# Block 1's attention products as float32r parts: scores and P V on the whole array, with half-height heads stacked as [hi;lo]

## The chip, the cores and the metric

The kernel runs on one core of one Trainium2 chip. The metric is device time in microseconds. The core's engines are TensorE (PE; its loads of stationary tiles are listed as PEld), VectorE (DVE), ScalarE (ACT), GpSimd (POOL) and SyncE (SP), which here only issues DMAs.

## The reference

Two transformer blocks are applied to 256 tokens of 1024 features, in float32. The first block has two layers on 272 positions (16 meta tokens and the 256 tokens). Each layer normalizes, projects once (`u @ w_in`), runs four branches and merges them behind sigmoid gates, then a gated convolutional feed-forward net. The branches that matter here, with T = 272:

```
A: 4 heads, 2 maps each:  s[m] = q[m] k[m]^T / 8 + bias      (64 features a map)
   a = softmax(s[0]) - lambda * softmax(s[1]);   o = a v       (v has 128 columns)
B: gated linear attention in chunks of 64
C: 4 heads:  s = (q_nope k_nope^T + q_pe k_pe^T) / sqrt(192)  (128 and 64 features)
   o = softmax(s) v                                            (128 columns)
D: 8 query heads on 2 key heads, window 128, meta tokens always seen, a sink
   s = q k^T / 8 + bias (64 features);   o = softmax(s) v      (64 columns)
```

The second block (two SwiGLU nets a layer, retention and dilated attention, stick-breaking attention) is not touched in its arithmetic.

## The kernel before

Features lie on partitions, tokens in the free dimension. A weight matrix comes from DRAM in pieces of 1 MB (`load`, three buffers `raw`). Each 128 columns of it are split into a pair: `hi` is an ACT copy to float32r, `lo` is a DVE subtraction of `hi` from the raw value (`split`, L209). A dense product is then three float32r products, hi x hi, hi x lo and lo x hi (`mm3`, L183), accumulated in a PSUM bank; a chunk of 128 columns over 1024 features is 24 of them. The pairs rotate through a ring of four buffers for hi and four for lo (pool `hip`, L1622), for the whole kernel.

In the first block the attention products are not split. Their operands are plain float32, and TensorE runs such a product as two instructions with the same tiles:

- scores of A (L675) and D (L774): a stationary tile of 64 rows by 128 queries, 272 keys; the two maps of a head (A), or the two heads of a chunk (D), lie in rows 0 to 63 and 64 to 127;
- scores of C (L888, L889): one product with 128 rows and one with 64;
- P V (`weighted`, L600): three products with 16, 128 and 128 keys; 128 output rows for A and C, 64 for D.

The weights P are normalized in SBUF (tile `E`), transposed on TensorE against an identity (L191), and copied by DVE into the tile `PT` (`transposed`, L574: a 128 x 512 copy, a 16 x 256 one, and two small ones for the 16 meta queries). The meta tokens' queries of all heads are packed in one tile and done once a branch (`meta_weights`, L588). Their biases `bmA` and `bmD` are loaded once, from POOL's queue (L424 to L426). The other biases come per head or chunk on SP's queue into a ring of three buffers, `B` (L668, L762). `PT` has two buffers (pool `ptp`, L1133). The values are transposed to tokens (`values`, L562): a 16 x 128 and a 128 x 256 DVE copy for each 128 columns; branch B uses the same function.

The order of the work is written in `layer1` (L1120): branch B, the projections of A and of C's latents, A's attention, the merge of B, the projections of D, C's up-projections and attention, the merge of A, D's attention, the merges of C and D. A planner then orders each engine's instructions by when they can start and when they are needed, so that dense products of one branch stand between the attention steps of another. Each engine, and each DMA queue, carries out its own list in order; waits are on semaphores.

Of the kernel before, what the change touches and what calls it, by code (L numbers as in the profile page):

```python
# [12 lines left out]
F32 = mybir.dt.float32  # L13
# [20 lines left out]
# column offsets in w_in  # L34
# [8 lines left out]
# token tiles of the first block: the meta tokens, then two tiles of 128  # L43
# [3 lines left out]
# constants that depend on shapes alone, one tensor; name -> (first column, columns)  # L47
# [25 lines left out]
def _constants():  # L73
# [63 lines left out]
    put(c2, "strictadd", np.where(t_ < s_, 0.0, NEG).astype(f))  # queries on partitions  # L137
# [18 lines left out]
    # relative positions: bucket table as one-hot columns for rel = 272 - i  # L156
# [10 lines left out]
class _Kernel:  # L167
# [69 lines left out]
    def newton(self, y, h, u, x, scale, eps):  # L237
        """y = (scale * x + eps) ** -0.5"""
# [3 lines left out]
        # a step of third order, without its factor of 1.5, then one of second order  # L242
# [8 lines left out]
    def after(self, last):  # L251
        """What this traces on the engines of the instructions `last` is issued after them."""
# [21 lines left out]
    def pairs(self, raw, kc, cw, slots=(), eng=None):  # L274
        """Stationary tiles of 128 columns, split: [(hi, lo)], each [128, kc, 128]."""
# [8 lines left out]
    def weights(self, w, c0, cw, kc=NK, slots=(), eng=None):  # L284
        """Columns c0..c0+cw of w [kc*128, n], split, by 128 columns."""
# [3 lines left out]
    def chunk(self, w, x, n, ps=None):  # L289
        """PSUM [128, n] = w^T x"""  # L290
# [6 lines left out]
    def chunks(self, ws, x, n):  # L297
        """PSUM [128, n] = w^T x for each w, all of them as x comes."""
# [7 lines left out]
    def stream(self, ws, x, n, first=3, more=0, total=None, rs=None):  # L306
        """PSUM tiles of w^T x in turn; the first ones follow x as it comes, some more use the scores' banks."""
# [11 lines left out]
    def setup(self):  # L319
# [15 lines left out]
        # gains and other vectors, as columns of 128  # L335
# [19 lines left out]
    def setup_vectors(self):  # L355
        """Gains, biases and convolutions' weights, as columns; the second call transposes most of them."""
# [58 lines left out]
    def setup_tables(self):  # L415
# [3 lines left out]
        # biases of the meta tokens' queries, packed: rows 32 * group + 16 * member + query  # L419
        self.bmA = cp.tile([P, T], F32, tag="bmA", name="bmA")  # L420
        self.bmD = cp.tile([P, T], F32, tag="bmD", name="bmD")
        for g in range(4):
            r = slice(32 * g, 32 * g + 32)
            nc.gpsimd.dma_start(self.bmA[r, :], self.toeplitz(g, 0, 16, 0, T, [4 * 544, 2]))  # L424
            nc.gpsimd.dma_start(self.bmD[r, T - 16 :], self.toeplitz(8 + g, 0, 16, 0, 16, [4 * 544, 2]))
            nc.gpsimd.dma_start(self.bmD[r, : T - 16], self.toeplitz(24 + g, 0, 16, 16, T - 16, [4 * 544, 2]))  # L426

        # lambda of the differential attention, sinks
# [23 lines left out]
        for l in range(2):  # L452
            # 1 for the first map's rows, -lambda for the second's
# [5 lines left out]
            self.sinkcol.append(lam[:, 2 + l : 3 + l])  # L459

# [20 lines left out]
    def add_square(self, total, a, first, eng):  # L481
        """total (+)= a * a"""
# [7 lines left out]
    def mean_rsqrt(self, total, n, width):  # L490
        """[128, n]: (mean over the features + eps) ** -0.5 in each row, from the sums by partition."""
# [38 lines left out]
    def postnorm(self, chunks, gain, l, h):  # L530
        """What does h[m] += rms_norm(f) * gain; chunks yields (m, PSUM of f's 128 features)."""
# [26 lines left out]
    # slots of [128, 4, T]; a tag's tiles are placed in the order of the program, so what may run ahead  # L558
    # has its own
# [40 lines left out]
    def weighted(self, out, V, c, w, PT):  # L600
# [1077 lines left out]
```

## Time and profile before

| | |
|---|---|
| time, median of 3 runs | 2298.96 us (2297.48 to 2299.21) |
| span of the profiled execution | 2293.8 us |
| profiled execution's own time | not listed beside its span |
| PE busy | 2220.7 us, 97%, 16925 instructions |
| PEld busy | 2081.1 us, 91% |
| DVE busy | 1672.1 us, 73% |
| ACT busy | 1069.5 us, 47% |
| POOL busy | 264.5 us, 12% |
| mean granted TensorE clock | 0.989 of full speed |

Busy time is the union of an engine's instructions. Matmuls are pipelined, so one starts before the one before it has ended; the distance from start to start is then what an instruction costs. The times of stretches are microseconds from the start of the span. The first layer's attentions lie between 140 and 420, its feed-forward net between about 430 and 640; the second layer's between 760 and 1040 and between about 1050 and 1250.

### The profile page before, as it was taken

How to read it: one execution, taken by the hardware profiler on the slowest of the kernel's cores; microseconds unless marked ns; L12 is line 12 of the kernel's file. 1: busy time of each engine (PE TensorE's matmuls, PEld its weight loads, DVE VectorE, ACT ScalarE, POOL GpSimd, SP SyncE). 2: the span in 40 equal slices, each digit the busy share in tenths (PEclk: the TensorE clock that was granted, in tenths of full speed). 3: DMA queues.
4: the chain of work that ended last, by engine and by line, in shares of the span. 5: the costliest groups of instructions: out<-in, count | busy, mean ns of one | idle time of the engine just before them, and what ended most of it. 6: DMA issues, size and time to landing. Idle time of an engine off the chain costs nothing.

```text
span 2293.8 us, 41993 instructions
## 1 busy us (share of the span) xinstructions
PE 2220.7 (97%) x16925; PEld 2081.1 (91%) x16925; DVE 1672.1 (73%) x3263; ACT 1069.5 (47%) x1678; POOL 264.5 (12%) x329
## 2 busy tenths in 40 slices
PE   8999999899979999998999999999999999999998
PEld 6989779899979898798999999988999999979997
DVE  7867676799488776768985774787774775687764
ACT  5243334566443433346664553444543554445543
POOL 5100112133031001121320000101000100101000
PEclk9999999999989999999999999999999999999999
DMA  7255336355533543464555555544555555524553
GB/s 211 93 137 164 96 106 176 129 184 179 176 115 92 150 148 111 106 205 158 187 175 175 166 185 184 176 139 132 186 187 183 179 185 184 183 99 151 187 190 119
DMA packets 300741, 360.61 MB, mean 157 GB/s; under 512 B 17382, under 2 KB 265444, under 8 KB 300420
## 3 DMA queue, kind: packets, MB, share of 16 engines
q1 hardware_dynamic: 298652, 354.38, 48.7%
q0 software_dynamic: 1664, 3.48, 0.5%
q8 instruction: 133, 2.18, 0.4%
q14 instruction: 60, 0.49, 0.1%
q10 hardware_dynamic: 232, 0.08, 0.0%
HBM read 354.63 MB, written 1.12 MB: 155 GB/s over the span
## 4 chain that ended last, share of the span: by engine, by line
PE 82%; DVE 10%; ACT 3%; issue 2%; DMA 2%; POOL 1%; SPq 0%; ACTq 0%; DVEq 0%; POOLq 0%
PE acc L181 57%; PE att L181 23%; PE att L191 2%; DVE lo L212 2%; ACT hi L207 1%; POOL total L488 1%; DVE xl L204 1%; DVE c L204 1%; DVE f L201 1%; DVE h L201 1%; ACT xh L207 1%; DVE b L201 1%; DMA raw<-in_w_in_dram 0%; DVE b L204 0%; DVE total L488 0%
## 5 line engine op out<-in xcount | busy, mean ns | idle before, releaser
L207 ACT ACTIVATE hi<-raw 128x1024 fp32r<-128x1024 f32 (+1 forms) x651 | 677.4, 1045 | 840.2 <-PE acc L181 632.1
L212 DVE TENSOR_TENSOR lo<-raw,hi 128x1024 fp32r<-128x1024 f32 (+1 forms) x649 | 803.0, 1241 | 286.8 <-ACT hi L207 280.1
L181 PE MATMUL acc<-xh,lo 128*128 128x256 f32 (+2 forms) x3312 | 951.9, 288 | 2.1 <-DVE lo L212 2.1
L181 PE MATMUL acc<-xh,hi 128*128 128x256 f32 (+2 forms) x3312 | 952.7, 288 | 0.6 <-ACT hi L207 0.5
L181 PE MATMUL acc<-xl,hi 128*128 128x256 f32 (+2 forms) x3312 | 947.1, 286 | 0.1
L181 PEld LDWEIGHTS acc<-xh,hi 128*128 128x128 f32 x3312 | 629.4, 190 | 10.9 <-issue 7.5
L181 PEld LDWEIGHTS acc<-xh,lo 128*128 128x128 f32 x3312 | 628.4, 190 | 11.6 <-issue 7.7
L181 PEld LDWEIGHTS acc<-xl,hi 128*128 128x128 f32 x3312 | 631.0, 191 | 6.7 <-issue 5.3
L181 PE MATMUL att<-ah,hi 128*128 128x256 f32 (+1 forms) x704 | 199.6, 283 | 0.0
L181 PE MATMUL att<-al,hi 128*128 128x256 f32 (+1 forms) x704 | 199.5, 283 | 0.0
L181 PE MATMUL att<-ah,lo 128*128 128x256 f32 (+1 forms) x704 | 199.5, 283 | 0.0
L488 POOL TENSOR_TENSOR total<-total,sq 128x256 f32<-128x256 f32 (+2 forms) x60 | 58.4, 973 | 815.1 <-ACT sq L207 812.4
L181 PEld LDWEIGHTS att<-ah,lo 128*128 128x128 f32 x704 | 134.5, 191 | 0.0
L181 PEld LDWEIGHTS att<-al,hi 128*128 128x128 f32 x704 | 134.5, 191 | 0.0
L181 PEld LDWEIGHTS att<-ah,hi 128*128 128x128 f32 x704 | 134.5, 191 | 0.0
L1118 POOL TENSOR_TENSOR merged<-merged,gate 128x272 f32<-128x272 f32 (+1 forms) x48 | 56.6, 1180 | 525.7 <-DVE small L904 275.4
L181 PE MATMUL acc<-ol,hi 128*128 128x272 f32 (+2 forms) x384 | 112.4, 293 | 1.1 <-DVE ol L212 1.1
L181 PE MATMUL acc<-oh,hi 128*128 128x272 f32 (+2 forms) x384 | 111.7, 291 | 0.0
L181 PE MATMUL acc<-oh,lo 128*128 128x272 f32 (+2 forms) x384 | 111.0, 289 | 0.0
L204 DVE SCALAR_TENSOR_TENSOR c<-u,vec,c 128x272 f32<-128x272 f32 (+1 forms) x176 | 105.5, 607 | 2.5
L201 DVE TENSOR_TENSOR u<-acc,rs 128x256 f32<-128x256 f32 (+2 forms) x171 | 72.4, 426 | 46.7 <-PE acc L181 46.4
L181 PEld LDWEIGHTS acc<-ol,hi 128*128 128x128 f32 x384 | 72.5, 189 | 8.1 <-issue 6.3
(370 smaller groups left out, 3104.3 us busy)
## 6 DMA issues: line engine op xcount, KB each, us to landing
raw<-in_ffn_w_in_dram SPq DMA_DIRECT2D x88, 1024.0 KB
raw<-in_w_in_dram SPq DMA_DIRECT2D x64, 1024.0 KB
raw<-in_ffn_w_up_dram SPq DMA_DIRECT2D x44, 1024.0 KB
raw<-in_ffn_w_out_dram SPq DMA_DIRECT2D x44, 1024.0 KB
raw<-in_ffn_w_down_dram SPq DMA_DIRECT2D x20, 1024.0 KB
raw<-in_hyb_w_in_dram SPq DMA_DIRECT2D x14, 1024.0 KB
raw<-in_w_branch_dram SPq DMA_DIRECT2D x12, 1024.0 KB
raw<-in_sb_w_in_dram SPq DMA_DIRECT2D x12, 1024.0 KB
```

Source lines behind the costliest of these rows:

```text
L181: self.last_mm = self.nc.tensor.matmul(ps, lhsT=lhsT, rhs=rhs, start=start, stop=stop, skip_group_check=True)
L191: return self.nc.tensor.transpose(ps, a, self.ident[:n, :n])
L201: self.nc.vector.tensor_tensor(out, a, b, op)
L204: return self.nc.vector.scalar_tensor_tensor(out, a, s, b, op0, op1)
L207: return self.nc.scalar.activation(out, a, f, **kw)
L212: (eng or self.nc.vector).tensor_tensor(lo, a, hi.bitcast(F32), ALU.subtract)
L488: self.last_add = eng.tensor_tensor(total, total, sq, ALU.add)
L1118: self.nc.gpsimd.tensor_tensor(merged[m], merged[m], x, ALU.add)
```

## The change

Scores and P V of A, C and D become products of float32r parts.

- A and D: a half-height operand of the queries is stored as a full-height tile [hi; lo] (`halves`), each head's or map's own rows holding hi and the other 64 rows lo. The keys are stored twice, as [hi; hi] and [lo; lo] (`doubled`). Two full-height products give all four parts of the score.
- C: `mm3` for the 128-row part, and two products for the rotary part, with [hi; lo] queries against the two tiles of the rotary key, which holds equal rows in both halves.
- P V: `transposed` now makes `ph` by an ACT copy and `pl` by a DVE subtraction; the 16 meta keys of P are stacked in an 80-row tile (hi in rows 0 to 15, and hi and lo in rows 32 to 47 and 64 to 79), whose other rows are zero. `weighted` is one product for the meta keys and `mm3` for each of two key tiles, seven in all. For D the values are put in tiles 128 columns wide whose other 64 columns are zero, and both heads of a chunk accumulate in one bank.
- `values` splits likewise; branch B keeps the old function under the name `plain_values`. `meta_weights` returns split weights.
- The meta queries' biases are no longer kept: `meta_bias` loads them in each layer, on SP's queue, into the ring `B`.
- Buffers: `hip` has three buffers in the first block and is opened again with four for the second. `P^T` (now `PH`, `PL`) has one buffer each, and so have the operand halves (`half_tile`). C's packed meta scores issue their four 128-row products first, then the 64-row ones.

Comments are dropped throughout. The core of the diff:

```diff
@@ transposed, weighted
+        ph, pl = (self.ptp.tile([P, 2, T], F32R, tag=f"P{t}", name=self.name("P" + t)) for t in "HL")
+        self.pm = self.pm[::-1]
+        pm = self.pm[0]
...
-        cp(PT[:, 1:3, 16:T], tp.rearrange("p (k q) -> p k q", k=2))
-        cp(PT[:16, 0, 16:T], t0[:16, 0:256])
-        cp(PT[:, 1:3, 0:16], meta[:, 64:192].rearrange("p (k g q) -> p k g q", k=2, g=4)[:, :, h])
-        cp(PT[:16, 0, 0:16], meta[:16, 16 * h : 16 * h + 16])
+        main = tp.rearrange("p (k q) -> p k q", k=2)
+        self.act(ph[:, :, 16:T], main, AF.Copy)
+        self.tt(pl[:, :, 16:T], main, ph[:, :, 16:T].bitcast(F32), ALU.subtract)
+        self.meta_rows(pm[:, 16:T], t0[:16, 0:256], "hi")
+        mh, ml = meta
+        cp(ph[:, :, 0:16], mh[:, 64:192].rearrange("p (k g q) -> p k g q", k=2, g=4)[:, :, h])
+        cp(pl[:, :, 0:16], ml.rearrange("p (k g q) -> p k g q", k=2, g=4)[:, :, h])
+        cp(pm[:, 0:16], mh[:80, 16 * h : 16 * h + 16])
...
-        for kt, (a, n) in enumerate(TILES):
-            self.mm(out, V[:n, kt, c : c + w], PT[:n, kt, :], kt == 0, kt == 2)
+        vh, vl, vm = V
+        ph, pl, pm = PT
+        self.mm(out, vm[:, cs], pm, start, False)
+        for kt in range(2):
+            self.mm3(out, (vh[:, kt, cs], vl[:, kt, cs]), (ph[:, kt], pl[:, kt]), False, stop and kt == 1)
@@ new helpers
+    def meta_rows(self, out, a, second):
+        self.act(out[0:16], a, AF.Copy)
+        hi, lo = (slice(32, 48), slice(64, 80))[:: 1 if second == "hi" else -1]
+        self.tt(out[lo], a, out[0:16].bitcast(F32), ALU.subtract)
+        self.act(out[hi], a, AF.Copy)
+    def half_tile(self, tag):
+        return self.mw.tile([P, T], F32R, tag=tag, name=self.name(tag), bufs=1)
+    def halves(self, a, tag):
+        out = []
+        for m in range(2):
+            r, o = slice(64 * m, 64 * m + 64), slice(64 - 64 * m, 128 - 64 * m)
+            t = self.half_tile(f"{tag}{m}")
+            self.act(t[r], a[r], AF.Copy)
+            self.tt(t[o], a[r], t[r].bitcast(F32), ALU.subtract)
+            out.append(t)
+        return out
+    def doubled(self, a):
+        out = []
+        for m in range(2):
+            r, o = slice(64 * m, 64 * m + 64), slice(64 - 64 * m, 128 - 64 * m)
+            hi, lo = self.half_tile(f"kd{m}"), self.half_tile(f"kl{m}")
+            self.act(hi[r], a[r], AF.Copy)
+            self.tt(lo[r], a[r], hi[r].bitcast(F32), ALU.subtract)
+            self.act(hi[o], a[r], AF.Copy)
+            self.act(lo[o], lo[r].bitcast(F32), AF.Copy)
+            out.append((hi, lo))
+        return out
@@ branch_a (branch_d likewise, with ks = self.doubled(K) once)
+            qs, ks = self.halves(Q[:, h], "qs"), self.doubled(K[:, h])
...
-                    self.mm(ps[:, :T], Q[64 * m : 64 * m + 64, h, a : a + P], K[64 * m : 64 * m + 64, h, :])
+                    for t in range(2):
+                        self.mm(ps[:, :T], qs[m][:, a : a + P], ks[m][t], t == 0, t == 1)
@@ branch_c
+        kr = self.half_tile("kl0"), self.half_tile("kl1")
+        self.split(*kr, KR)
...
+            if h % 2 == 0:
+                qr = self.halves(QR[:, h // 2], "qr")
+            qn, kn = (tuple(self.half_tile(f"{tag}{n}") for n in range(2)) for tag in ("qs", "kd"))
+            self.split(*qn, QN[:, h])
+            self.split(*kn, KN[:, h])
...
-                self.mm(ps[:, :T], QN[:, h, a : a + P], KN[:, h], True, False)
-                self.mm(ps[:, :T], QR[r0 : r0 + 64, h // 2, a : a + P], KR[r0 : r0 + 64, :], False, True)
+                self.mm3(ps[:, :T], [q[:, a : a + P] for q in qn], kn, True, False)
+                for t in range(2):
+                    self.mm(ps[:, :T], qr[h % 2][:, a : a + P], kr[t], False, t == 1)
@@ branch_a, branch_d
-        self.neg_scores(em, ps[:, :T], self.bmA[:, ::-1], sm[:, 0:1])
+        self.neg_scores(em, ps[:, :T], self.meta_bias(0, False), sm[:, 0:1])
@@ layer1, run
-            self.ptp = self.pool(st, f"ptp{l}", 2, reuse_waits="tile")
+            self.ptp = self.pool(st, f"ptp{l}", 1, reuse_waits="tile")
-        self.hip = self.pool(ctx, "hip", 4)
+            self.hip = self.pool(block, "hip", 3, reuse_waits="tile")
+        self.hip = self.pool(ctx, "hip2", 4, reuse_waits="tile")
```

## Rows read from the trace of the kernel before

**Rows 1.** The page: span, and busy us (share of the span) xinstructions.

```profile
span 2293.8 us, 41993 instructions
...
PE 2220.7 (97%) x16925; PEld 2081.1 (91%) x16925; DVE 1672.1 (73%) x3263; ACT 1069.5 (47%) x1678; POOL 264.5 (12%) x329
```

**Rows 2.** Stretches: start:end length, busy PE, PEld, DVE, ACT, POOL, clock, DMA, GB/s.

```profile
140.00:187.00 47.00, 46.53 (x276) 34.80 (x276) 37.61 (x137) 22.24 (x53) 0.00 (x0) 1.00 0.49 121
760.00:805.00 45.00, 45.00 (x291) 34.88 (x290) 35.20 (x126) 21.77 (x51) 0.00 (x0) 1.00 0.52 137
...
140.00:420.00 280.00, 278.69 (x1905) 236.90 (x1905) 196.81 (x523) 118.07 (x224) 29.38 (x26) 1.00 0.47 136
760.00:1040.00 280.00, 277.22 (x1952) 235.93 (x1951) 198.51 (x529) 116.99 (x224) 28.17 (x25) 1.00 0.50 145
420.00:640.00 220.00, 207.62 (x1623) 205.67 (x1622) 177.32 (x270) 123.58 (x193) 54.17 (x59) 0.99 0.52 170
```

**Rows 3.** PE's old products: groups (busy us, mean ns), then P V's ns min/median/max.

```profile
L181 PE MATMUL att<-dk,b 64*128 64x272 f32 x64 | 17.6, 441 | 0.0
L181 PE MATMUL att<-b,b 64*128 64x272 f32 x64 | 16.7, 441 | 0.5 <-DVE small L613 0.5
L181 PE MATMUL att<-kr,b 64*128 64x272 f32 x32 | 11.6, 441 | 0.0
L181 PE MATMUL att<-b,b 128*128 128x272 f32 x32 | 10.7, 415 | 0.0
...
L181 PE MATMUL att<-PT,V x192: 387/393/497, 162.1 to 971.3; 128*128 128x272 f32 x64, 128*64 128x272 f32 x64, 16*128 16x272 f32 x32, 16*64 16x272 f32 x32
```

**Rows 4.** Timeline of PE in A's attention: start us, length us, instruction, count.

```profile
163.86 0.72 PE L181 MATMUL att<-b,b 64*128 64x272 f32 x2
...
167.49 1.84 PE L181 MATMUL att<-PT,V 16*128 16x272 f32 x6
169.25 0.73 PE L181 MATMUL att<-b,b 64*128 64x272 f32 x4
169.91 0.39 PE L181 MATMUL acc<-xh,lo 128*128 128x272 f32 x1
170.14 0.29 PE L181 MATMUL acc<-xh,hi 128*128 128x272 f32 x1
...
171.15 0.29 PE L181 MATMUL acc<-xh,lo 128*128 128x272 f32 x1
```

**Rows 5.** Timeline of PE in D's attention, one block of P V.

```profile
318.50 1.73 PE L181 MATMUL att<-PT,V 16*64 16x272 f32 x6
```

**Rows 6.** Groups of ACT and DVE: count, then busy us, mean ns, idle before.

```profile
L207 ACT ACTIVATE b<-merged 128x272 fp32r<-128x272 f32 x8 | 3.5, 432 | 16.8 <-POOL merged L1118 16.8
L1038 ACT COPY b<-att 128x512 f32<-128x512 f32 x8 | 4.7, 585 | 18.3 <-PE att L181 18.3
...
L201 DVE TENSOR_TENSOR gate<-acc,rs 128x272 f32<-128x272 f32 x32 | 13.9, 434 | 16.7 <-PE acc L181 16.7
L212 DVE TENSOR_TENSOR lo<-raw,hi 128x512 fp32r<-128x512 f32 x20 | 13.1, 688 | 0.8 <-ACT hi L207 0.6
L583 DVE COPY PT<-att 128x512 f32<-128x512 f32 x32 | 22.1, 690 | 12.6 <-PE att L191 12.4
L585 DVE COPY PT<-metaw 128x32 f32<-128x32 f32 x32 | 5.2, 162 | 0.0
```

**Rows 7.** Timelines of PE, ACT and DVE in the conv stage, about one pair.

```profile
504.01 0.29 PE L181 MATMUL acc<-xh,hi 128*128 128x272 f32 x1
...
504.64 1.04 ACT L207 ACTIVATE hi<-raw 128x1024 fp32r<-128x1024 f32 x1
...
506.11 1.73 DVE L212 TENSOR_TENSOR lo<-raw,hi 128x1024 fp32r<-128x1024 f32 x1
```

**Rows 8.** SP's waits (us, times, longest); the chain's longest bias landing in A's stage.

```profile
SPq L668 <- DVE small L613: 29.1, 5, 9.9
...
153.56 4.40 DMA B<-rel
```

More of the change, by code (lines that the diff above doesn't have):

```diff
@@ L459, in setup_tables, with meta_bias @@
             self.sinkcol.append(lam[:, 2 + l : 3 + l])
+    def meta_bias(self, row, masked):
+        b = self.bp.tile([P, 2, T], F32, tag="B", name=self.name("B"))[:, 0]
+        for g in range(4):
+            r = slice(32 * g, 32 * g + 32)
+            if masked:
+                self.nc.sync.dma_start(b[r, T - 16 :], self.toeplitz(row + g, 0, 16, 0, 16, [4 * 544, 2]))
+                self.nc.sync.dma_start(b[r, : T - 16], self.toeplitz(row + 16 + g, 0, 16, 16, T - 16, [4 * 544, 2]))
+            else:
+                self.nc.sync.dma_start(b[r, :], self.toeplitz(row + g, 0, 16, 0, T, [4 * 544, 2]))
+        return b[:, ::-1]
     def k(self, name):
@@ L560, with token_values, zeros, values @@
     SLOTS = {"b4": 8, "E": 2, "ms": 1, "oh": 1, "ol": 1}
-    def values(self, V, c, ps, rs, n):
+    def token_values(self, ps, rs):
+        vt = self.mw.tile([P, T], F32, tag="vt", name=self.name("vt"))
+        self.tt(vt, ps, rs, ALU.mult)
+        tp = self.att()
+        for j in (1, 2, 0):
+            a, w = TILES[j]
+            self.transpose(tp[:w, (j + 2) % 3 * P : ((j + 2) % 3 + 1) * P], vt[:, a : a + w])
+        return tp
+    def meta_rows(self, out, a, second):
[3 more added lines that the diff above has]
+        self.act(out[hi], a, AF.Copy)
+    def zeros(self, pool, shape, tag, **kw):
+        t = pool.tile(shape, F32R, tag=tag, name=self.name(tag), **kw)
+        self.nc.gpsimd.memset(t.bitcast(F32), 0.0)
+        return t
+    def values(self, V, c, ps, rs):
+        tp = self.token_values(ps, rs)
+        cs = slice(c * P, (c + 1) * P)
+        main = tp[:, : 2 * P].rearrange("p (j v) -> p j v", j=2)
+        self.act(V[0][:, :, cs], main, AF.Copy)
+        self.tt(V[1][:, :, cs], main, V[0][:, :, cs].bitcast(F32), ALU.subtract)
+        self.meta_rows(V[2][:, cs], tp[:16, 2 * P : 3 * P], "lo")
+    def plain_values(self, V, c, ps, rs):
         vt = self.mw.tile([P, T], F32, tag="vt", name=self.name("vt"))
@@ L572, in values, with split_values, transposed @@
         )
-    def transposed(self, PT, e2, meta, h):
+    def split_values(self):
+        hi = self.vp.tile([P, 3, 512], F32R, tag="V", name=self.name("VH"))[:, 0:2]
+        lo = self.vp.tile([P, 3, 512], F32R, tag="V", name=self.name("VL"))[:, 0:2]
+        return hi, lo, self.zeros(self.mw, [80, 512], "VM", bufs=1)
+    def transposed(self, e2, meta, h):
         cp = self.nc.vector.tensor_copy
+        ph, pl = (self.ptp.tile([P, 2, T], F32R, tag=f"P{t}", name=self.name("P" + t)) for t in "HL")
+        self.pm = self.pm[::-1]
+        pm = self.pm[0]
         tp, t0 = self.att(), self.att()
@@ L733, in branch_d @@
         ps = self.chunk(W[1], xs, T)
-        self.values(V, 0, ps[:, :T], rs, T)
+        vs = self.big4("b4", F32R).rearrange("p h t -> p (h t)")[:, 0 : 8 * P].rearrange("p (s i k v) -> p s i k v", s=2, i=2, k=2)
+        nc.gpsimd.memset(vs.bitcast(F32), 0.0)
+        vm = self.zeros(self.mw, [80, 2, P], "VMD", bufs=1)
+        tp = self.token_values(ps[:, :T], rs)
+        V = []
+        for i in range(2):
+            c = slice(64 * i, 64 * i + 64)
+            main = tp[:, : 2 * P].rearrange("p (j v) -> p j v", j=2)[:, :, c]
+            self.act(vs[:, 0, i, :, c], main, AF.Copy)
+            self.tt(vs[:, 1, i, :, c], main, vs[:, 0, i, :, c].bitcast(F32), ALU.subtract)
+            self.meta_rows(vm[:, i, c], tp[:16, 2 * P + 64 * i : 2 * P + 64 * i + 64], "lo")
+            V.append((vs[:, 0, i], vs[:, 1, i], vm[:, i]))
         yield
-        QM = self.mw.tile([P, 4, 32], F32, tag="QM", name=self.name("QM"))
+        QM = self.mw.tile([P, 4, 32], F32, tag="QM", name=self.name("QM"), bufs=1)
         nc.gpsimd.memset(QM, 0.0)
@@ L754, in branch_d @@
             metas.append(self.meta_weights(em, self.k("selA"), r))
+        ks = self.doubled(K)
         O = self.big4()
@@ L768, in branch_d @@
                 nc.vector.tensor_copy(sk[:, 2 * i : 2 * i + 2], self.sink[l][:, c + 4 * i : c + 4 * i + 1].to_broadcast([P, 2]))
+            qs = self.halves(Q[:, c], "qs")
             for j in range(2):
@@ L870, in branch_c @@
         for h in range(4):
+            self.mm(ps[32 * h : 32 * h + 32, :T], QN[:, h, 0:32], KN[:, h], True, False)
+        for h in range(4):
             r0 = 64 * (h % 2)
-            self.mm(ps[32 * h : 32 * h + 32, :T], QN[:, h, 0:32], KN[:, h], True, False)
             self.mm(ps[32 * h : 32 * h + 32, :T], QR[r0 : r0 + 64, h // 2, 0:32], KR[r0 : r0 + 64, :], False, True)
@@ L894, in branch_c @@
                 nc.vector.tensor_scalar(E[:, j], E[:, j], sm[:, 8 + j : 9 + j], None, ALU.mult)
-            PT = self.ptp.tile([P, 3, T], F32, tag="PT", name=self.name("PT"))
-            self.transposed(PT, (E[:, 0], E[:, 1]), meta, h)
+            PT = self.transposed((E[:, 0], E[:, 1]), meta, h)
             ps = self.att()
-            self.weighted(ps[:, :T], V, h * P, P, PT)
+            self.weighted(ps[:, :T], V, slice(h * P, (h + 1) * P), PT)
             nc.vector.tensor_copy(O[:, h], ps[:, :T])
@@ L1132, in layer1 @@
             self.bp = self.pool(st, f"bp{l}", 3, reuse_waits="tile")
-            self.ptp = self.pool(st, f"ptp{l}", 2, reuse_waits="tile")
+            self.ptp = self.pool(st, f"ptp{l}", 1, reuse_waits="tile")
             self.mw = self.pool(st, f"mw{l}", 2, reuse_waits="tile")
+            self.pm = [self.zeros(self.mw, [80, T], f"pm{n}", bufs=1) for n in range(2)]
             ob, KR = self.branch_b(l, w, xs, rs)
```

49 lines of the change are left out of this document (21 added, 28 removed).

## The prediction

> **What bounds the kernel now.** I read the page's busy shares first, then a table of stretches for the attention stages, the groups by line and shape of TensorE, and timelines. The reader is to see, in this order: TensorE (PE) is busy for 2220.7 of 2293.8 us [rows 1]; in both stretches that hold the attentions of the first block PE is busy for 278.7 and 277.2 of 280 us, with VectorE (DVE) at 197 and 199 and ScalarE (ACT) at 118 and 117 [rows 2]. There is no wait to remove in these stages: the planner already fills the gaps between attention steps with dense products. So the change is worth what it takes from PE's own work, less what it makes PE wait for.
>
> The sum is made against the profiled execution, whose span is 2293.8 us; the median of the three runs, 2298.96, lies 5.2 us above that span, and I carry this difference over.
>
> **What goes from PE.** The old products of the scores fall in four groups, those of P V have one row [rows 3]. An fp32 product is two instructions. A score block, of one half-height product or of two, is busy for 0.72 or 0.73 us, and the next instruction starts 0.66 us after it (169.25, 169.91) [rows 4]. The busy time thus holds a tail that the next one overlaps, and 0.66 / 0.73 = 0.90 of it is PE's. The four groups are 17.6 + 16.7 + 11.6 + 10.7 = 56.6 us busy, so 51.0 us. Of P V there are 192 instructions in blocks of six, 32 products: a full one takes 1.76 us, from 167.49 to 169.25, 0.08 less than its busy time [rows 4], a half-width one of D 1.73 - 0.08 = 1.65 us [rows 5]; 16 x 1.76 + 16 x 1.65 = 54.6 us. Removed: 105.6 us.
>
> A dense product costs 0.126 us a start (170.14 to 171.15 in eight steps), but the one behind an fp32 block takes 0.23 us (169.91 to 170.14) [rows 4], 0.10 more. There are some 90 blocks ((56.6 - 10.7) / 0.73 = 63 of scores, where C's full-height ones join the half-height ones, and 32 of P V, some of them joined), not all before a dense product: between 0 and 9 us. I take 4, since many meet another attention block or a transpose, which stays fp32.
>
> **What comes to PE.** Per layer: scores of A 16 x 2, of D 16 x 2, of C 8 x (3 + 2), together 104; P V is 7 products each for 4 heads of A, 4 of C and 8 of D, 112. In two layers that is 432 with 272 columns. Their nearest row is the dense float32r product of the same shape, 0.126 us: 54.4 us. The other bound is the one after a switch, 0.23: 99 us. I take 0.126, since two to seven of them stand in a row and their neighbours are of the same kind. The 80-row product of the meta tokens is priced like the others; there are 32, so even at 0.33 (the longest step in the old blocks, 0.66 / 2) it would add 7 us.
> PE's balance: 105.6 + 4 - 54.4 = 55 us less.
>
> The Trainium skill, TensorEngine Tiling (Array Packing), "When to Use Tiling", speaks against one half of this: with a contraction of at most 64 rows the array works as two half-height tiles side by side, which stacking [hi;lo] on all 128 rows gives up. The rows show such pairs: four instructions cost the same 0.66 us as two [rows 4]. By the rule alone the 64 half-height products of A and D would have been 32 pairs, 21 us; the rows have 34.3 us busy, 31 us of PE, so the pairing often failed, and the trace decides.
>
> **What comes to ACT and DVE.** Rows for the price: a 128 x 272 ACT copy of fp32r kind 0.432 us, a 128 x 512 ACT read of a bank 0.585; DVE's 128 x 272 two-operand step 0.434, its 128 x 512 subtraction 0.688, the 128 x 512 copy that it replaces 0.690, a small copy 0.162 [rows 6]. Half-height and narrower ones I price like the full ones of the nearest width, which can only be too much.
> Copies of operands, per layer: A 4 x (2 + 6) ACT and 4 x 4 DVE; D 6 + 8 ACT and 2 + 8 DVE; C 13 and 13. That is 59 ACT and 39 DVE, in both layers 51 and 34 us. The transposed weights: 32 times 0.585 + 2 x 0.432 = 1.45 us of ACT, 46 us; on DVE subtractions replace copies of equal price, and one small copy comes, 5 us. Values and meta weights: 84 small ACT copies in both layers, at 0.432 at most 36 us, 28 by estimate since most are 16 partitions high and 128 wide or less. So ACT gets about 125 us and DVE about 39, half in each layer.
> Over a whole stretch that fits: DVE 197 + 20 = 217 and ACT 118 + 62 = 180, against 279 - 27 = 252 of PE. Within A's attention it doesn't: there DVE has 37.6 of 47 us and ACT 22.2 [rows 2]. A's share of the new work is 16 x 0.434 + 4 x 0.162 = 7.6 us of DVE, which makes 45.2, and 4 x (8 x 0.432 + 1.45) = 19.6 of ACT, 41.8; PE falls by A's part (16.7 x 0.90 / 2 + 4 x 1.76 - 60 x 0.126 = 7.0) to 39.5. DVE becomes the last one there, 5.7 us over; in the second layer 42.8 against 38.0, 4.8 us. Bounds for this: 0 (the planner moves other dense work in: the merge of B and the projections of D don't depend on A) and 10 us. I take 7, nearer to the upper, since ACT is short at the same place.
>
> **Buffers and queues.** The transposed weights and the operand halves have one buffer each where the old P^T had two. So the copies of a head's operands wait for the last scores of the head before, and those of P^T for its P V. Next to them dense products run, as now; I add 4 us for what this order costs, between 0 (dense work covers it) and 10 (two waits of 0.585 + 0.69 us at each of the 8 heads of A, half of them covered).
> The ring of split weights in the first block goes from four pairs to three. In the conv stage, where DVE is at 177 of 220 us [rows 2], ACT writes the pair two chunks ahead 0.63 us after the chunk before has ended (a chunk starts at 504.01, the copy at 504.64), and its subtraction ends at 507.84, 2 us before that chunk begins (two chunks of 24 x 0.126 = 3.0 us later, 510.0) [rows 7]. So three pairs are live at a time, and the fourth isn't needed: between 0 and 10 us, I take 4.
> The bias rows of the meta queries leave Pool and come to SP, 12 issues a layer. Behind them on SP stand weight loads. SP already waits for bias buffers there, 29.1 us in 5 waits of A's loads [rows 8], while PE stays full [rows 2]: the weights loaded ahead are the cover. Nothing to 9 us; I take 0. With the cover gone, A's stage would start one landing later, 4.40 us in the chain [rows 8], in each layer.
>
> **Sum.** 2293.8 - 55 + 7 + 4 + 4 = 2253.8 of span, with 5.2 around it **2259 us**, 1.7% faster.
>
> **Rivals.**
> 1. *The longer chain is exposed.* The P^T of a head is copied by ACT, then subtracted by DVE, then used, with a single buffer: if all 32 show their 1.45 us of ACT, 46 us come in place of my 15, and the time is 2290. For it: DVE at 37.6 of 47 us in A's stage. Against it: PE stands full in these stages with chains of this kind, and ACT is free for more than half of each stretch [rows 2].
> 2. *The ring of three starves PE, slower than before.* Place: conv-up and down of both layers, 128 split pairs (in the code, a layer has 44 of w_up, less 2 held elsewhere, and 22 of w_down), where DVE is at 177 of 220 us [rows 2] and a split that waits for a release can miss its turn. If each pair comes late by the 0.63 us that now separates release and copy, PE loses 81 us: 2340. It decides against the change from 40 / 128 = 0.31 us a pair. Against it: the 2 us lead above.
> 3. *The products don't get their price.* If each of the 432 costs what a switched one does, 0.23 us, 45 us of the gain go: 2304. For it: attention blocks are short and stand between fp32 transposes. Against it: in the nine dense ones after a block only the first is long [rows 4].
>
> **Chances.** Forecast 0.72, the first rival 0.14, the second 0.08, the third 0.06. The forecast's own range is 2239 (no losses, 9 of switches) to 2275; the first rival carries the upper end to 2292. About 0.2% (4.6 us) is what can be told from no change. Faster: 0.72 + 0.13 = 0.85; the rest of rival 1 and part of 3 make 0.04 for no change; slower 0.11.
>
> **What would show it.** Right: PE's instructions with P^T and half-height operands gone, 432 new ones with starts 0.125 us apart; the spans of 140 to 420 and 760 to 1040 shorter by 20 us or more each; PE's idle time in them under 10 us. The conv stages unchanged within 3 us, else the ring matters. Wrong: PE idle in A's stage behind the new ACT copies or DVE subtractions for more than 10 us a layer (rival 1), waits of ACT's weight copies on PE that now stop PE in conv (rival 2), steps of 0.2 us inside the new blocks (rival 3).

## The result and the profile after

The changed kernel takes 2316.3 us (median of four runs, 2312.2 to 2319.1) beside 2298.2 us of the kernel before on the same chip: a ratio of 1.0079, 95% interval 1.0065 to 1.0093. It is slower by 18 us, where 2259 was forecast; the forecast's range ended at 2292. (Medians, here and below, are of all runs of a kernel. A ratio with its interval is worked out from the single runs of both kernels, and can lie up to some 0.1% beside the quotient of the medians.)

The page of the changed kernel, span and busy shares (answers to [rows 1]):

```profile
span 2310.4 us, 42449 instructions
...
PE 2200.5 (95%) x16973; PEld 2105.7 (91%) x16973; DVE 1712.6 (74%) x3377; ACT 1182.0 (51%) x1976; POOL 263.9 (11%) x337
```

The same stretches as in [rows 2], columns as there:

```profile
140.00:187.00 47.00, 40.87 (x259) 35.95 (x258) 37.79 (x133) 35.05 (x87) 0.21 (x1) 0.89 0.49 115
760.00:805.00 45.00, 42.77 (x311) 38.71 (x310) 32.93 (x98) 26.80 (x58) 0.21 (x1) 0.96 0.50 146
140.00:420.00 280.00, 264.36 (x1956) 247.65 (x1955) 219.24 (x579) 167.37 (x355) 29.77 (x37) 0.98 0.51 139
760.00:1040.00 280.00, 264.52 (x1989) 246.26 (x1988) 221.66 (x589) 162.01 (x352) 26.71 (x30) 0.96 0.52 144
420.00:640.00 220.00, 207.54 (x1612) 205.94 (x1610) 168.95 (x258) 125.72 (x194) 51.73 (x50) 0.98 0.51 163
```

From 140 to 420 TensorE was busy for 278.7 of 280 us before, and is for 264.4 now: the attention no longer fills it, and its granted clock is under 1 there (0.98, and 0.96 in the second layer).

The new products, first as groups (the columns of [rows 3]: busy us, mean ns, idle before), then two P V blocks of D on the timeline (answers to [rows 4, 5]):

```profile
L181 PE MATMUL att<-kd,qs 128*128 128x272 f32 x112 | 34.7, 346 | 7.8 <-ACT kd L207 2.8 <-DVE small L695 2.1 <-ACT em L207 1.7
L181 PE MATMUL att<-kl,qs 128*128 128x272 f32 x64 | 21.1, 333 | 3.1 <-ACT kl L207 3.0
L181 PE MATMUL att<-PH,b 128*128 128x272 f32 x64 | 14.6, 288 | 0.0
```

```profile
313.50 0.29 PE L181 MATMUL att<-pm,VMD 80*128 80x272 f32 x1
313.63 0.28 PE L181 MATMUL att<-PH,b 128*128 128x272 f32 x1
...
314.26 0.28 PE L181 MATMUL att<-PH,b 128*128 128x272 f32 x1
314.38 0.60 PE L191 MATMUL att<-ident,E 128*128 128x128 f32 x4
...
319.54 0.40 PE L181 MATMUL att<-pm,VMD 80*128 80x272 f32 x1
319.77 0.29 PE L181 MATMUL att<-PH,b 128*128 128x272 f32 x1
...
320.52 0.60 PE L191 MATMUL att<-ident,E 128*128 128x128 f32 x4
```

The seven products of the first block take 0.88 us from the first to what follows them, 0.126 each, where the old block took 1.65 [rows 5]. The second block is the usual one: its 80-row product is followed only after 0.23 us, and the block takes 0.98, which is the median of all 32. The price of the products is as forecast but for the one that opens a block.

What TensorE waited for, over the whole program (engine, tile and line, waited for: us, times, longest us):

```profile
PE acc L181 <- ACT xh L207: 21.4, 4, 7.1
PE acc L181 <- DVE lo L212: 12.7, 22, 1.4
PE att L181 <- DVE total L491: 12.1, 6, 4.0
...
PE acc L181 <- ACT hi L207: 6.2, 8, 1.8
PE att L181 <- ACT pm L207: 5.2, 8, 1.5
...
PE att L181 <- ACT kl L207: 3.0, 3, 1.5
PE att L181 <- ACT kd L207: 2.8, 5, 1.3
```

The same two kinds of weight waits in the kernel before:

```profile
PE acc L181 <- DVE lo L212: 4.6, 5, 1.6
...
PE acc L181 <- ACT hi L207: 0.9, 2, 0.5
```

So, over the whole program, dense products (acc) wait 18.9 us for the hi and lo parts of weights, where it was 5.5; beside that stand the waits of attention products for the new copies (pm, kl, kd), 11.0 us.

The trace can be cut at instructions that both kernels have: the first product of A's meta scores (start of "A"), the first 64-row product of C's meta scores, the first product of conv-up, and of the next dense stage. The lengths in us, and those of the experiments that the next section tells of (ring: slots of split weights in the first block; "moved" is opened where the change opens it; A, C and D cover whatever dense work the planner put among them):

| kernel | to A | A | C, D | conv | B | A | C, D | conv | rest |
|---|---|---|---|---|---|---|---|---|---|
| before | 143.6 | 88.3 | 197.6 | 212.9 | 129.7 | 86.4 | 193.1 | 202.6 | 1039.6 |
| changed | 146.3 | 94.0 | 188.5 | 221.2 | 136.5 | 92.2 | 186.5 | 204.0 | 1041.2 |
| before, ring of 4 moved | 144.3 | 88.3 | 197.6 | 213.2 | 131.4 | 86.2 | 192.9 | 204.1 | 1040.5 |
| before, ring of 3 | 146.4 | 89.1 | 202.5 | 217.4 | 134.7 | 86.2 | 196.9 | 203.8 | 1041.1 |
| P V alone, ring of 4 | 145.2 | 89.2 | 184.0 | 215.9 | 133.7 | 89.5 | 180.5 | 204.0 | 1040.0 |
| changed, ring of 4 | 144.4 | 96.3 | 178.3 | 215.0 | 132.4 | 95.7 | 173.1 | 202.5 | 1043.4 |
| the same, A's scores old | 144.8 | 89.9 | 177.9 | 215.1 | 132.5 | 90.4 | 174.7 | 202.5 | 1043.6 |

In the changed kernel C and D are shorter by 9.1 and 6.6 us, A is longer by 5.7 and 5.8, and the stages with no attention in them (to A, conv, B, conv) are longer by 2.7, 8.3, 6.8 and 1.4.

### The profile page after: what moved, and what is told of

Read it like the earlier page. It is cut to its first block, busy times and chain, and to the rows that moved or that the text cites. A ratio compares the mean times of both kernels' runs of the same rounds, so it can differ in the third digit from the quotient of the medians.

```text
span 2310.4 us, 42449 instructions
## 1 busy us (share of the span) xinstructions
PE 2200.5 (95%) x16973; PEld 2105.7 (91%) x16973; DVE 1712.6 (74%) x3377; ACT 1182.0 (51%) x1976; POOL 263.9 (11%) x337
## 4 chain that ended last, share of the span: by engine, by line
PE 75%; DVE 12%; ACT 7%; issue 3%; DMA 2%; POOL 1%; SPq 0%; ACTq 0%; DVEq 0%; POOLq 0%
PE acc L181 53%; PE att L181 20%; DVE lo L212 3%; ACT hi L207 3%; PE att L191 2%; POOL total L491 1%; DVE xl L204 1%; DVE f L201 1%; DVE h L201 1%; ACT E L207 1%; DMA B<-rel 1%; ACT xh L207 1%; DVE c L204 1%; ACT kd L207 0%; ACT b L207 0%
## 5 line engine op out<-in xcount | busy, mean ns | idle before, releaser
L212 DVE TENSOR_TENSOR lo<-raw,hi 128x1024 fp32r<-128x1024 f32 (+1 forms) x649 | 791.6, 1223 | 310.6 <-ACT hi L207 303.2
L1222 POOL TENSOR_TENSOR merged<-merged,gate 128x272 f32<-128x272 f32 (+1 forms) x48 | 51.3, 1069 | 348.3 <-DVE gate L204 214.1
```

The lines of the kernel that those rows point to most:

```text
L1222: self.nc.gpsimd.tensor_tensor(merged[m], merged[m], x, ALU.add)
```

## The experiments

Two theories stood at the start. T1: the operand copies on ACT and DVE hold TensorE up. T2: the ring of split weights, which went from four slots to three, costs outside the attention.

**The ring alone.** The kernel before with only this edit:

```diff
-        self.hip = self.pool(ctx, "hip", 4)
+            self.hip = self.pool(block, "hip", 3, reuse_waits="tile")
...
+        self.hip = self.pool(ctx, "hip2", 4, reuse_waits="tile")
```

> The kernel before with one edit: the ring of split weights has three buffers in the first block and is opened again with four for the second. Theory T1 (the operand copies and split P^T on ACT and DVE starve PE in the attention stages, and the lower clock that follows costs the rest): 0 to 4 us over before. Theory T2 (outside the attention stages 20.8 us were lost, 2.7 in layer 0's first stage, 6.8 in layer 1's, 8.3 and 1.4 in the conv stages, 1.6 later, and the ring is the cause): 15 to 21 us over before, PE idle 8 us more in the first conv stage and layer 1's branch B.

Measured: 2326.2 us, ratio 1.0127 (1.0110 to 1.0144): 27 us slower, with not one attention product changed, and more than T2's 15 to 21.

**Half of the change each, at the ring of three.** First P V by the new products and the scores as before:

```diff
-                    for t in range(2):
-                        self.mm(ps[:, :T], qs[m][:, a : a + P], ks[m][t], t == 0, t == 1)
+                    self.mm(ps[:, :T], Q[64 * m : 64 * m + 64, h, a : a + P], K[64 * m : 64 * m + 64, h, :])
```

> The changed kernel with the scores of A, C and D as before (plain fp32, no operand copies); P V, values, ring of three, bias loads and buffers as in the change. P V's products give 54.6 - 28.2 = 26 us of PE. T1: without the 118 ACT copies and 78 DVE subtractions of operands the idle time in the attention stages falls from 41 us to under 20 in both layers and the clock stays up: 2275 to 2285. T2: the 20 us outside the attentions stay, 2290 to 2300.

Measured: 2322.2 us, 1.0105 (1.0090 to 1.0120), above what either theory had. Then the scores by the new products and P V as before (the first diff turned round, P^T and V as in the kernel before):

> The kernel before with the scores part alone, the ring of three and the bias loads per layer; P V, P^T and values as before. Scores give 51.0 - 26.2 = 25 us of PE. T1: the copies cost more idle time and clock than they give, 2300 to 2320, most of it in A's attention. T2: 2290 to 2300, as with P V alone.

Measured: 2340.1 us, 1.0179 (1.0164 to 1.0194): above both theories, and 14 us above the ring alone. Its A stages are 99.7 and 97.9 us long, 10.6 and 11.7 more than the ring's; its stages of C and D are 195.7 and 191.8, 6.8 and 5.1 less.

**The copies of operands, at the ring of three.**

```diff
-            qs, ks = self.halves(Q[:, h], "qs"), self.doubled(K[:, h])
+            if h == 0:
+                qs, ks = self.halves(Q[:, h], "qs"), self.doubled(K[:, h])
```

and likewise in C and D.

> The changed kernel without the operand copies of the heads and chunks after the first (C's rotary queries after the first pair too): their scores use the first head's split operands, so the products are as many, and the computed scores of those heads are another's. Left out are 4/5 of the copies in both layers. T1: PE idle and low clock in A's attention go, the kernel loses 25 to 40 us against the changed one, 2276 to 2291. T2: 5 to 10 us less than the changed one.

Measured: 2315.3 us, 1.0072 (1.0057 to 1.0087), as the changed kernel; T2's 5 to 10 us less did not come either. T1 in its simple form falls: with most copies gone, nothing is won at a ring of three.

**The ring's size or its place?** The ring of four, opened where the change opens it:

```diff
-            self.hip = self.pool(block, "hip", 3, reuse_waits="tile")
+            self.hip = self.pool(block, "hip", 4, reuse_waits="tile")
```

> The kernel before with its ring of hi and lo weight tiles kept at four, but allocated inside the first block and opened again after it, as the change does (only the size differs from the kernel with the ring of three alone, which took 2326.2 us beside 2298.9 of the kernel before). Theory T2 (the size of the ring costs: with one weight pair less split ahead, TensorE waits at the ends of the norms): 2295 to 2302 us. Rival T3 (it is where and how the ring is opened, not its size): 2315 to 2330 us.

Measured: 2303.3 us, 1.0023 (1.0012 to 1.0034), 1 us above T2's range and far under T3's. So the place is worth 4.8 us and the size 23 (2326.2 less 2303.3). What TensorE waited for up to the end of the second layer's conv stage, first with four slots, then with three:

```profile
PE acc L181 <- ACT xh L207: 14.8, 3, 4.9
...
PE att L181 <- DVE total L488: 7.5, 4, 2.6
...
PE acc L181 <- DVE lo L212: 2.6, 3, 1.6
```

```profile
PE acc L181 <- ACT xh L207: 16.9, 3, 7.1
PE att L181 <- DVE total L488: 9.0, 5, 3.3
...
PE acc L181 <- DVE lo L212: 7.3, 12, 1.4
...
PE acc L181 <- ACT hi L207: 3.4, 4, 1.4
```

Waits for lo come 12 times in place of three, and for hi four times in place of one. Up to there TensorE is idle for 12.7 us more (61.1 beside 48.4), of which lo and hi are 7.8, and busy for 6.4 us more (1216.0 beside 1209.7) with as many instructions. One place where the slot is missed is the start of B in the second layer, on ACT's timeline. With four slots (its first dense product starts at 643.4):

```profile
653.06 0.73 ACT L207 ACTIVATE sq<-h 128x272 f32<-128x272 f32 x2
653.70 1.04 ACT L207 ACTIVATE hi<-raw 128x1024 fp32r<-128x1024 f32 x1
662.25 2.01 ACT L207 ACTIVATE hi<-raw 128x1024 fp32r<-128x1024 f32 x2 [7.52 <-PE acc L181]
```

and with three (the first product at 655.4):

```profile
665.05 0.73 ACT L207 ACTIVATE sq<-h 128x272 f32<-128x272 f32 x2
672.68 2.01 ACT L207 ACTIVATE hi<-raw 128x1024 fp32r<-128x1024 f32 x2 [6.90 <-PE acc L181]
```

With four, ACT splits one more pair the moment the norm's squares are done, at 10.3 us; with three it stands for 6.9 us, until TensorE lets a slot go, and its first split is at 17.3 us. In the stage table the 19.6 us between these two spans lie for the most part outside conv: 2.1 to A, 0.8 in A, 4.9 in C and D, 4.2 in conv, 3.3 in B, 4.0 in C and D of the second layer, -0.3 in its conv, 0.6 in the rest.

Two things come with the ring of three that are not waits for its pairs. Half of conv's 4.2 us is the longest wait for xh, at the norm before B, 7.1 us in place of 4.9: there one VectorE instruction takes 2.29 us (first line; the second is the same one at the next norm). It does so in the six kernels with three slots and three raw tiles, and in none of the others; why isn't shown.

```profile
648.93 2.29 DVE L240 TENSOR_SCALAR n<-nt 128x9 f32<-128x9 f32 x1
...
668.24 0.17 DVE L240 TENSOR_SCALAR n<-nt 128x9 f32<-128x9 f32 x1
```

And the planner's order is another. Counted from A's first meta score, TensorE has done 940 dense products before D's last P V block of the first layer, in the kernel before and with the ring moved alike, but 917 with three slots. The 23 us are thus the slot's with the order made for it; no run takes the two apart.

**Pairs or loads?** The ring of three with one more tile for raw weights:

```diff
-        self.rawp = self.pool(ctx, "rawp", 3)
+            self.rawp = self.pool(block, "rawp", 4, reuse_waits="tile")
...
+        self.rawp = self.pool(ctx, "rawp2", 3, reuse_waits="tile")
```

> The kernel before with the ring of hi and lo tiles at three in the first block (2326.2 us by itself) and the pool of raw weights at four there, in place of three. Theory T2a (what the ring of three loses is split pairs ready ahead of a norm's end; one more load ahead doesn't replace a pair): 2320 to 2328 us. Rival T2b (a raw tile comes free only when its pair has a slot, so the loads are late): 2298 to 2312 us.

Measured: 2319.5 us, 1.0102 (1.0072 to 1.0131). T2b falls: a load more ahead gives back at most a part of the 23 us. Conv of the first layer goes from 217.4 to 214.2 us, of which 2 are the VectorE instruction above, which takes its usual time here; C and D stay. So loads are not what is short; the pairs, or the order that comes with three of them, cost the rest.

**P V alone, with the ring of four.** The P V half as above, with the ring as in the moved one.

> P V by the new products, the scores as before, the ring at four in the first block (with the ring of three this took 2322.2 us). Theory T2: 2322 less the 27 us of the ring alone, 2292 to 2298 us. Rival T3: 2318 to 2325 us, unchanged. Rival T4, that the new products lose by themselves: 2300 to 2310 us.

Measured: 2284.0 us, 0.9930 (0.9913 to 0.9946): 38 us under the same kernel with three slots, 19 under the ring of four by itself, and under every theory's range. This half of the change is a gain at four slots; at three it was 4 us (2326.2 to 2322.2), with intervals that overlap.

**The changed kernel with a ring of four.** Room has to be found for the fourth slot:

```diff
-        hi = self.vp.tile([P, 3, 512], F32R, tag="V", name=self.name("VH"))[:, 0:2]
+        vh = self.vp.tile([P, 3, 512], F32R, tag="V", name=self.name("VH"))
+        hi, vm = vh[:, 0:2], vh[:80, 2]
...
-        G = self.mw.tile([32, T], F32, tag="glat", name=self.name("glat"), bufs=1)
+        G = self.mw.tile([P, T], F32, tag="em", name=self.name("glat"), bufs=1)[:32]
...
-                x = self.mw.tile([P, T], F32, tag="gate", name=self.name("gate"))[:, :nt]
+                x = self.mw.tile([P, T], F32, tag="vt", name=self.name("gate"), bufs=3)[:, :nt]
...
-            self.hip = self.pool(block, "hip", 3, reuse_waits="tile")
+            self.hip = self.pool(block, "hip", 4, reuse_waits="tile")
```

> The changed kernel with a ring of four in the first block: the room for it comes from putting the meta tokens' values into the unused third of the tile of V's hi part, and from sharing five small tiles (gate, swap and vt in one ring of three, the latent gate in em's place, AU in a bias tile). Theory T2 (the ring's size is what the change loses): 2316 less the 27 us of the ring alone, 2285 to 2295 us, faster than both. Rival T3 (where it is opened): 2311 to 2320, unchanged. Rival T4 (the attention's new stages lose most by themselves, through waits for the split operands and the lower granted clock): 2303 to 2312.

Likewise swap takes a buffer of vt's three, and AU one of the bias tiles. Measured: 2280.8 us, 0.9922 (0.9907 to 0.9937): faster than both, by 17.7 us than the kernel before and by 35.5 than the changed one, and than T2's range. The control with the shared tiles and three slots:

> The control of the changed kernel with a ring of four: the same shared tiles with the ring of three. All theories: 2312 to 2322 us, as the changed kernel; if the shared tiles cost by themselves it is above that.

Measured: 2307.5 us, 1.0030 (1.0011 to 1.0050), 8.8 us under the changed kernel, which no theory had said. So of the 35.5 us the slot is 26.7 and the sharing 8.8. The sharing in the kernel before, as far as it has these tiles:

> The kernel before with the ring of four opened in the first block (2303.3 us) and the same small tiles shared as in the changed kernel with a ring of four: gate, swap and vt in one ring of three, the latent gate in em's place, AU in a bias tile. If the sharing changes nothing in itself: 2299 to 2307 us, and the new products' gain at a ring of four is some 22 us. If it is the sharing that made the changed kernel with shared tiles and a ring of three 8.8 us faster than the changed kernel: 2292 to 2297 us.

Measured: 2301.1 us, 1.0020 (1.0005 to 1.0034), 2.2 us under the same without it: the sharing is no gain of its own worth the name there, and the 8.8 us stay unexplained. Between the changed kernel and the control the stages of C and D get 5.0 and 5.5 us shorter, those of A 2.9 longer, and the order is another here too (838 dense products before D's first P V block, 815 with the shared tiles): a candidate that no run tests. TensorE's waits for lo and hi in the changed kernel with four slots (12.7 and 6.2 us with three, above):

```profile
PE acc L181 <- DVE lo L212: 4.0, 4, 1.6
...
PE acc L181 <- ACT hi L207: 2.5, 3, 1.8
```

**A's scores.** In the stage table the changed kernel with four slots is shorter in C and D than P V alone (178.3 to 184.0 and 173.1 to 180.5: 5.7 and 7.4 us), but 7.1 and 6.2 us longer in A. It also has the shared tiles, which P V alone has not. A's scores as before, all else as there (the edit shown for P V alone, in A only):

> The changed kernel with the ring of four (2280.8 us) and A's scores as in the kernel before; C's and D's scores and all P V by the new products. Theory T5 (in A's stage the chain of DVE and ACT is the bound once TensorE needs less, so A's new scores buy nothing there and add operand copies to it; the stage was 96.3 and 95.7 us with them against 89.2 and 89.5 with P V alone): 7 us a layer back and what A's scores saved lost nowhere else, 2266 to 2274 us. Rival T6 (the new scores pay in A as in C and D, the longer A stage is only work moved between stages): 2284 to 2292, A's saving of some 4 us a layer gone.

Measured: 2270.4 us, 0.9865 (0.9836 to 0.9893), 10.4 us under the one with A's new scores. T5 holds in its number, and this is the best kernel of the study: 28 us under the kernel before. The loss is one of this kernel. At the ring of three, with tiles not shared, the changed kernel has A stages of 94.0 and 92.2 us and P V alone 91.6 and 93.9, and all the new scores together are a gain of 5.9 us (2322.2 to 2316.3).

T5 said that the softmax's chain is the cause, not the copies. All the operand copies but the first head's left out, at four slots:

> The changed kernel with the ring of four, in which only the first head's (chunk's) score operands are split and copied; the other heads' scores use the first's, so their products are the same number with other data. Theory T1 (the copies on ACT and DVE are what TensorE waits for in A's stage): A's stage back to some 89 us, 2265 to 2273 us. Theory T5 (the softmax's chain on DVE and ACT, which is there without them, is the bound): 2276 to 2283 us, A's stage still above 92 us.

Measured: 2272.2 us, 0.9882 (0.9852 to 0.9912): T1's number for the whole, but not T1's place. A's stage is 94.2 us in the first layer, above T5's 92, and 91.7 in the second. So the same with A's copies alone left out:

> The changed kernel with the ring of four (2280.8 us) in which, in A alone, only the first head's score operands are split and copied, the other heads' products use them. If A's loss of 10.4 us (with its new scores 2280.8, with its old ones 2270.4) is its operand copies: 2272 us or less. If it is the softmax's chain, bare once TensorE is faster there, as T5 has it: 2278 to 2282 us. Without the copies and with no other loss, A's scores would save 7 us: 2264.

Measured: 2276.5 us, 0.9914 (0.9890 to 0.9939), between the two expectations. By the medians 4.3 of the 10.4 us come back, by the ratios (0.9922 and 0.9914) 2, and the intervals overlap: that is not clear of noise. In A's stages, 94.8 and 90.9 us, 1.5 of 6.4 come back in the first layer and 4.8 of 5.3 in the second. The first layer's first stretch of A (columns of [rows 2]) with A's new scores, then without their copies, then with the old scores:

```profile
140.00:187.00 47.00, 40.27 (x273) 35.61 (x272) 38.78 (x137) 35.27 (x88) 0.47 (x2) 0.93 0.48 111
```

```profile
140.00:187.00 47.00, 40.94 (x272) 35.74 (x271) 37.17 (x137) 26.59 (x68) 1.89 (x4) 0.93 0.50 119
```

```profile
140.00:187.00 47.00, 46.91 (x310) 37.72 (x309) 39.18 (x135) 27.63 (x68) 0.64 (x2) 1.00 0.57 139
```

Without the copies ACT has 9 us less to do, yet TensorE is busy for the same 41 us, at a granted clock of 0.93. What it waits for from 144 to 190, with the copies and then without:

```profile
PE att L181 <- ACT kd L207: 2.3, 4, 0.9
PE att L181 <- ACT pm L207: 1.7, 2, 1.5
PE att L181 <- ACT kl L207: 1.5, 2, 1.1
PE att L181 <- DVE small L697: 1.2, 1, 1.2
```

```profile
PE att L181 <- DVE small L697: 2.0, 2, 1.1
PE att L181 <- ACT pm L207: 1.8, 2, 1.2
PE att L191 <- DVE E L204: 1.7, 2, 1.4
```

The waits for kd and kl go, and the softmax's own steps (small, E) take their place: with the new scores TensorE is through before the scores have been turned into weights. So both parts of the cause are there. Which is the larger isn't shown: the first layer speaks for the chain, the second for the copies.

**ACT's load or the chain's length?** K's second copies on GpSimd:

```diff
-            self.act(hi[o], a[r], AF.Copy)
-            self.act(lo[o], lo[r].bitcast(F32), AF.Copy)
+            self.nc.gpsimd.tensor_copy(hi[o], a[r])
+            self.nc.gpsimd.tensor_copy(lo[o], lo[r].bitcast(F32))
```

> The changed kernel with the ring of four, the second copies of K's halves (hi and lo onto the other 64 partitions) made by GpSimd in place of ScalarE, in A and D. If TensorE waits for ScalarE's copies because ScalarE is full at that place, 2274 to 2279 us; if what counts is the length of the chain copy, subtraction, copy, 2281 or more, since GpSimd's copies are not shorter.

Measured: 2278.5 us, 0.9927 (0.9901 to 0.9953). This lies in the first theory's range, but beside the 0.9922 with ScalarE's copies nothing can be told from it; the question stays open.

## Why the prediction was wrong

Put together from the medians: before 2298.5; the ring of four moved, +4.8; P V with the change's bias loads and single buffers, -19.3; C's and D's scores, -13.6; A's scores, +10.4; that is the 2280.8 of four slots (the step to C's and D's scores holds the sharing of tiles too). Without the fourth slot, +26.7, and with the tiles not shared, +8.8, that makes 2316.3. The steps hang on their order: along the runs at three slots they are +27.4 for the ring, -4.0 for P V and -5.9 for all the scores, which gives the same 2316.3.

- *The failing step* is "three pairs are live at a time, and the fourth isn't needed: between 0 and 10 us, I take 4". It cost 23 us on the old products, 26.7 on the new, and 38 with P V alone. The reading that it rested on [rows 7] was nearly right for its stage: the two conv stages lose 4.2 and -0.3 us. Wrong was to read one steady stage for a ring that serves the whole block: 15.1 of the 19.6 us between the two profiled executions lie in the first block's other stages, at its starts and in C and D. The shortage shows in the waits for lo and hi and in the late first split at B; how much is the other order is open. Opening the ring in the block, +4.8, stood in no term.
- *The second rival*, that the ring starves TensorE, had the side right, and place and price wrong: conv, at 0.31 us a pair or more, where the runs show 3.9 us for the 128 pairs of both stages, 0.03 a pair. *The first rival*, the longer chain of P^T, shows in TensorE's waits with 5.2 us for pm and 0.3 for PL, far from its 46.
- *The products* held: 0.126 us a product behind a block's first, and the third rival is out. At four slots P V saved 19.3 us where the working has 54.6 - 28.2 = 26.4; C's and D's scores, with the sharing, 13.6 where it has 35.9 - 18.1 = 17.8. The 32 blocks of P V take 30.8 us there from their first product to what follows, so 2.6 of the 7.1 us missing from P V are the products that open a block. The rest, with the 4 us forecast for dense products behind fp32 blocks, answers to the term for single buffers and order (+4); no run took these apart. As the sharing was worth 8.8 us elsewhere, C's and D's scores may be worth less than 13.6. With tiles not shared, at three slots, the new scores leave the stages of C and D 6.8 and 5.1 us shorter on the old P V and 3.3 and 4.0 on the new.
- *A's stage* was named rightly as the place where ACT and DVE come last, and mis-sized: +7 in both layers was set against a saving of 15.0 - 64 x 0.126 = 6.9 us by A's scores, so nothing lost on balance. Measured at four slots, the scores lose 10.4: a cost of 17 where the forecast has 7, and the copies, the chain that follows the scores and the lower clock share it in parts that no run settles. The sum of DVE's and ACT's busy time against the stage's length was no guide to that: DVE is at 38.8 of 47 us there, never full. That the length of steps which follow each other is what is in the way is a reading of the waits; the run that was to tell length from load did not.
- *ACT and DVE* got 112.5 and 40.5 us more (125 and 39 forecast). That the copies are half as high or narrower saves them little, as the rows of the changed kernel show:

```profile
L207 ACT ACTIVATE kd<-b 64x272 fp32r<-64x272 f32 x32 | 13.7, 428 | 3.3 <-PE att L181 1.7 <-DVE b L201 1.0
L207 ACT ACTIVATE kd<-b 128x272 fp32r<-128x272 f32 x8 | 3.4, 420 | 0.1
L207 ACT ACTIVATE pm<-att 16x256 fp32r<-16x256 f32 x64 | 23.6, 369 | 21.2 <-PE att L191 10.7 <-DVE pm L201 9.8
```

  Half the height is 428 ns beside 420, and a 16-row copy 369. So the height doesn't count in the kd rows. From the 1.04 us of a 128 x 1024 copy [rows 7] and the 0.420 of 272 columns, the 752 columns between them cost 0.62 us, so 272 cost 0.22, and an estimated 0.2 us of each copy from SBUF is there whatever its width. The Trainium skill, VectorE: DVE Perf Modes, "The TRN2 errata", says that VectorE and ScalarE pay a fixed latency per instruction on operands from SBUF, so that many small tiles each pay it; the trace agrees with these 0.2 us for ScalarE.
- *The granted clock* stood in no term. In A's two stretches it was 1.00 before [rows 2]; it is 0.89 and 0.96 in the changed kernel, where TensorE is busy for 40.9 of 47 and 42.8 of 45 us, and 1.00 again with A's old scores and four slots, at 46.9 and 44.0. The stage of B in the second layer, where the attention isn't, differs too:

```profile
642.30:772.00 129.70, 120.20 (x895) 113.90 (x895) 104.91 (x201) 51.39 (x64) 22.25 (x23) 0.95 0.35 105
```

```profile
650.00:786.50 136.50, 127.75 (x895) 120.13 (x895) 106.92 (x204) 56.86 (x83) 22.26 (x23) 0.88 0.34 97
```

```profile
634.00:766.40 132.40, 122.36 (x896) 115.90 (x896) 107.95 (x205) 58.24 (x84) 22.85 (x24) 0.94 0.35 103
```

  That is the kernel before, the changed one, and the changed one with four slots: 895 or 896 instructions of TensorE in each, at 0.95, 0.88 and 0.94 of the clock. Of all the kernels here those with three slots have 0.88 to 0.90 in this stage and those with four 0.89 to 0.95. With the ring alone changed it is 0.92 with four slots, opened in the block, and 0.90 with three, so the ring is not all of it. With three slots a long stretch of the stage stands mostly at the lower of the two levels, 1.2 GHz (the kernel before with the ring of three):

```profile
696.10:723.40 27.30, 24.10 (x134) 21.08 (x133) 19.85 (x33) 5.26 (x7) 2.81 (x2) 0.56 0.13 39
```

- *SP's bias loads*, costed at nothing, were not tried by themselves. VectorE, which uses the biases, waits for them for 2.9 us in the changed kernel and 2.4 before. But in the chain of work that ended last stand three bias landings of the first block, 5.48, 2.57 and 5.02 us, where the kernel before has one of 4.40 [rows 8]: their price is open.

Still open: the 8.8 us of the shared tiles, what the planner's order has in the slot's price, and how the 17 us of A's stage divide among the copies, the chain and the lower clock.

## What to carry to other kernels

When a change pays for its buffers with a slot of a shared ring, price that slot by itself: run the old kernel with the smaller ring. Look for its use in every stage that the ring serves, at norms and stage ends too, and not in one steady loop, where the lead looked ample here. And a stage in which one engine is full while the chain beside it is nearly as long may give nothing back when that engine gets faster: here, at four slots, the same edit made the stages of C and D shorter and lost in A. Parts of a change also hang on each other: P V alone was worth 4 us with three slots and 19 with four.

## What was not expected of the hardware

A ring slot that the second layer's conv stage doesn't miss was worth 23 to 38 us of 2300, though with the ring alone changed the longest of TensorE's waits for its pairs was 1.4 us. One VectorE instruction of 0.17 us took 2.29 in all kernels with three slots but the one with four raw tiles. And short waits came with a lower clock. In A's first stretch with the new scores TensorE was busy for 40.3 of 47 us and its granted clock a mean 0.93, a part of the time at the lower of its two levels, 1.2 GHz; with the old scores it was busy for 46.9 of 47, at 1.00.
